# A Hyena block's transform step by half-height fp32 products from a turned x1

## The chip, the cores and the metric

The kernel runs on one core of a Trainium2 chip. The metric is the device time of one execution in microseconds (us). The engines are TensorE (PE), VectorE (DVE), ScalarE (ACT), GpSimd (POOL) and SyncE (SP, which issues DMAs here).

## The reference

One encoder layer on x of 2048 tokens by 1024 channels, all in float32. After an RMSNorm one projection gives 7168 columns, which feed two branches of 1024 channels:

```
a = c_val * sigmoid(c_gate);  a = depthwise conv of 31 taps over tokens
a = silu(layernorm per 128 channels(a)) * silu(c_z)
x0, x1, v = three depthwise convs of 3 taps
y = long_conv(v * x1) + skip;  y = rmsnorm per 128 channels(y * x0) * silu(hy_z)
out = rmsnorm(x + [a, y] @ w_out)
```

The long convolution is done by a transform of length 4096 in two steps. Its first step, the subject here, turns 2048 tokens, read as 64 rows n1 by 32 columns n2, into 32 vectors of 128 (64 real, 64 imaginary parts): for each n2, a product of a 64-row matrix of cosines and sines with the 64 tokens of that n2.

## The kernel before

A float32 product is written as three products of a faster format, fp32r: both operands are split into a high and a low part, and high by high, high by low and low by high are summed in PSUM (`chunk`, lines 235 to 237). 24 such products make one 128 by 512 output tile, here called a chunk, and four chunks (`inproj`) make one block of 128 projection columns for all tokens.

After the norm and the filters, phase A (about 400 to 1500 us) goes through eight groups of 128 channels. In turn i of its loop: `conf_glu(i)` projects value and gate (8 chunks) and writes the product into the buffer `apad`; `conf_taps(i)` runs the 31-tap convolution on DVE as 30 instructions of 128x2048 (line 541), given out a few at a time by `some(n)`; `conf_norm` centres the group before by products with `ctr` (lines 562 and 563, high and low part, which wait for ACT's L556 and DVE's L557) and gathers variances by four products on 32 columns of the array each (`vp`, line 569); `hyena(i - 1)` projects x1 and v, runs their short convolutions (`short_conv`: one ACT instruction L619, two DVE ones L621 and L622 per 512 tokens) and multiplies them (L640). Their sum `s` is a 128x2048 tile with tokens in order.

Then `stage1(i - 1)` does the transform's first step. It is a generator: `chunk` asks it for a step at two places of every chunk, while x0 and then the next gate are projected. A step takes the 64 tokens of a column n2 with a stride of 32, transposes them on PE (L662, four columns per PSUM bank), makes a high part by an ACT copy (L664) into partitions 0 to 63 and a low part by a DVE subtraction (L665) into partitions 64 to 127, and multiplies the stack by the 128-row matrix `st1`, in high and low part (L678, L679). ACT evicts the result (L681) and SP stores it to `AU` (L682).

The PSUM tiles `aux` (transposes, step results, centring) share three buffers, `mm` (chunks) has four; `apad` and `ppad` have one each. Each engine works through its own queue in order; a scheduler of the framework sets that order when the kernel is built, so it doesn't follow from the code alone. The view `turned` (tokens laid out column n2 by column) exists already for x0 and for the gate `hz`.

Of the kernel before, what the change touches and what calls it, by code (L numbers as in the profile page):

```python
# [11 lines left out]
F32 = mybir.dt.float32  # L12
F32R = mybir.dt.float32r
AF = mybir.ActivationFunctionType
# [4 lines left out]
P = 128  # L19
# [4 lines left out]
TC = 512  # L24
NT = L // TC
# [6 lines left out]
N1, N2 = 128, 32  # L32
# [27 lines left out]
def _split(m):  # L60

    m = np.asarray(m, np.float32)
    b = m.view(np.uint32)
    hi = ((b + np.uint32(0x7FF) + ((b >> np.uint32(12)) & np.uint32(1))) & np.uint32(0xFFFFF000)).view(np.float32)
    return hi, m - hi


def _constants():

    f32 = np.float32  # L70
    t = np.linspace(0.0, 1.0, L).astype(f32)
    bands = (EMB - 1) // 2
    w = f32(2.0 * math.pi / L) * np.arange(L, dtype=f32)
    f = np.linspace(1e-4, bands - 1, bands).astype(f32)
    fw = (f[None, :] * w[:, None]).astype(f32).astype(np.float64)
    z = np.concatenate([t[:, None], np.cos(fw).astype(f32), (-np.sin(fw)).astype(f32)], axis=1)

    fwd = np.empty((N2, 64), np.int64)
    bwd = np.empty((N2, 64), np.int64)
    for n2 in range(N2):  # L80
        fwd[n2] = 32 * np.arange(64) + n2
        bwd[n2] = 32 * (np.arange(64) + 1) - n2
    bwd[0, 63] = 0
    zf = np.concatenate([z[fwd.ravel()].T, z[bwd.ravel()].T], axis=0)
    tn = np.concatenate([-t[fwd].T, -t[bwd].T], axis=0)

    n1 = np.arange(N1)[:, None]
    k1 = np.arange(64)[None, :]
    ang = np.pi * (2 * k1 + 1) * n1 / 128.0
    e1 = np.concatenate([np.cos(ang), -np.sin(ang)], axis=1)  # L90
    s1u = np.concatenate([e1[:64], e1[:64]], axis=0)
    s1k = np.concatenate([e1[:64], -e1[128 - np.arange(1, 65)]], axis=0)
    s1k0 = s1k.copy()
    s1k0[127] = e1[0]
    st1 = np.stack([x for m in (s1u, s1k, s1k0) for x in _split(m.astype(f32))], axis=1)

    st2 = np.zeros((NPAIR, P, 8, P), f32)
    n2 = np.arange(N2)[:, None]
    k2 = np.arange(N2)[None, :]
    for p in range(NPAIR):  # L100
        m = np.zeros((2, 2, N2, 2, 2, N2))
        for l in range(2):
            kk = l * 32 + p
            g = np.exp(-1j * np.pi * ((2 * kk + 1) * n2 / 4096.0 + k2 * n2 / 16.0))
            m[0, l, :, 0, l, :] = g.real
            m[1, l, :, 0, l, :] = -g.imag
            m[0, l, :, 1, l, :] = g.imag
            m[1, l, :, 1, l, :] = g.real
        m = m.transpose(2, 0, 1, 3, 4, 5).reshape(P, P)
        re, im = m[:, :64], m[:, 64:]  # L110
        for j, x in enumerate((m, m.T, np.concatenate([re, re], axis=1), np.concatenate([-im, im], axis=1))):
            st2[p, :, 2 * j], st2[p, :, 2 * j + 1] = _split(np.ascontiguousarray(x).astype(f32))

    a = np.pi * (2 * np.arange(64)[:, None] + 1) * np.arange(64)[None, :] / 128.0
    inv = np.concatenate([np.cos(a), -np.sin(a)], axis=0) * (2.0 / 4096.0)
    sel = np.zeros((P, NT, P))
    for j in range(NT):
        sel[32 * j, j] = 1.0
        sel[32 * j + 16, j] = 1.0
    part = np.arange(P) % 32 >= 16  # L120
    ctr = np.eye(P) - np.full((P, P), 1.0 / P)
    return {
        "c_z": np.ascontiguousarray(zf),
        "c_t": np.ascontiguousarray(tn),
        "c_st1": np.ascontiguousarray(st1),
        "c_st2": st2,
        "c_inv": inv.astype(f32),
        "c_sel": sel.astype(f32),
        "c_part": np.stack([np.where(part, -1.0, 1.0), np.where(part, 1.0, 0.0)], axis=1).astype(f32),
        "c_ctr": ctr.astype(f32),  # L130
    }
# [39 lines left out]
def hybrid_kernel(ctx: ExitStack, tc: tile.TileContext, A, out):  # L171
    nc = tc.nc
    mm = nc.tensor.matmul
# [3 lines left out]
    AU = dram.tile([P, N2 + 1, D], F32, name="AU")  # L177
# [7 lines left out]
    cst = ctx.enter_context(tc.tile_pool(name="cst", bufs=1, reuse_waits="tile"))  # L185
# [6 lines left out]
    ident = cst.tile([P, P], F32, name="ident")  # L192
# [5 lines left out]
    nc.vector.memset(ones_g, 1.0 / P)  # L198
    ctr = cst.tile([P, P], F32R, name="ctr")
    sel = cst.tile([P, NT, P], F32R, name="sel")  # L200
    st1 = cst.tile([P, 2, P], F32R, name="st1")

# [37 lines left out]
    with ExitStack() as c0:  # L242
        hzp = c0.enter_context(tc.tile_pool(name="hzp", bufs=2, reuse_waits="tile"))
        ps = c0.enter_context(tc.tile_pool(name="ps0", bufs=1, space=PSUM, reuse_waits="tile"))
# [77 lines left out]
        for i, k in ((1, EMB), (2, FO), (3, FO)):  # L322
            w = kp.tile([2 * k, P], F32, name=f"fw{i}")
# [8 lines left out]
        for c in range(2):  # L332
# [2 lines left out]
            nc.sync.dma_start(wo_raw, A["filt_wo"][:, cs])  # L335
            nc.vector.tensor_copy(woh[:, cs], wo_raw)
            nc.vector.tensor_sub(wol[:, cs], wo_raw, woh[:, cs].bitcast(F32))
        for to, name, w in ((ctr, "c_ctr", P), (sel.rearrange("p a b -> p (a b)"), "c_sel", NT * P),
                            (st1.rearrange("p a b -> p (a b)"), "c_st1", 2 * P)):
            raw = kp.tile([P, TC], F32, name="dec", bufs=2)[:, :w]  # L340
            src = A[name] if name == "c_ctr" else A[name].rearrange("p a b -> p (a b)")[:, :w]
            nc.sync.dma_start(raw, src)
            nc.vector.tensor_copy(to, raw)
        stk = kp.tile([P, 4, P], F32R, name="stk")
        sk_raw = kp.tile([P, 4, P], F32, name="dec", bufs=2)
        nc.sync.dma_start(sk_raw, A["c_st1"][:, 2:6])
        nc.vector.tensor_copy(stk, sk_raw)

        def mlp(t):
# [107 lines left out]
    def tmp(dt=F32, shape=(P, TC)):  # L457
        return wk.tile(list(shape), dt, name="t", bufs=NTMP)
# [39 lines left out]
    with ExitStack() as c0:  # L498
        ps = c0.enter_context(tc.tile_pool(name="psA", bufs=1, space=PSUM, reuse_waits="tile"))
# [92 lines left out]
        def turned(x):  # L592

            return x.rearrange("p (n2 n1) -> p n1 n2", n2=N2)
# [18 lines left out]
        def short_conv(co, a, j, turn=False):  # L613
            n = TC

            def v(x):
                return x.rearrange("p (a b) -> p a b", b=N2) if turn else x

            nc.scalar.activation(co, v(ppad[:, a + 1:a + 1 + n]), AF.Identity, bias=sm("sh_b", j),  # L619
                                 scale=sm("sh_w", 3 * j + 1))  # L620
            nc.vector.scalar_tensor_tensor(co, v(ppad[:, a:a + n]), sm("sh_w", 3 * j), co, op0=OP.mult, op1=OP.add)  # L621
            nc.vector.scalar_tensor_tensor(co, v(ppad[:, a + 2:a + 2 + n]), sm("sh_w", 3 * j + 2), co,  # L622
                                           op0=OP.mult, op1=OP.add)

        def x1_out(i, some):
            s = long()

            def conv(t):
                short_conv(s[:, t * TC:(t + 1) * TC], t * TC, 8 + i)
                some(1)  # L630

            short_in(32 + i, after=conv)
            return s

        def gated(s, i, some):
            def conv(t):
                ts = slice(t * TC, (t + 1) * TC)
                c = tmp()
                short_conv(c, t * TC, 16 + i)
                nc.vector.tensor_mul(s[:, ts], s[:, ts], c)  # L640

            short_in(40 + i, after=conv)

# [10 lines left out]
            return c  # L654

        def stage1(i, s, some):
            sv = s.rearrange("p (n1 n2) -> p n2 n1", n2=N2)

            def turn(q):
                tp = ps.tile([64, 4, P], F32, name="aux", bufs=3)  # L660
                for r in range(4):
                    nc.tensor.transpose(tp[:, r], sv[:, 4 * q + r], ident)  # L662
                S = tmp(F32R, (P, 4, P))
                nc.scalar.activation(S[:64], tp, AF.Copy)  # L664
                nc.vector.tensor_sub(S[64:], tp, S[:64].bitcast(F32))  # L665
                return S

            for _ in range(STAGE1_WAIT):
                yield
            S = [turn(0)]  # L670
            yield
            S.append(turn(1))
            yield
            for q in range(8):
                if q < 6:
                    S.append(turn(q + 2))
                so = ps.tile([P, 4, P], F32, name="aux", bufs=3)
                mm(so, st1[:, 0], S[q], start=True, stop=False)  # L678
                mm(so, st1[:, 1], S[q], start=False, stop=True)  # L679
                sb = tmp(F32, (P, 4, P))  # L680
                nc.scalar.activation(sb, so, AF.Copy)  # L681
                nc.sync.dma_start(AU[:, 4 * q:4 * q + 4, i * P:(i + 1) * P], sb)  # L682
                if q % 2:
                    some(1)
                yield

        def hyena(i, some):
# [6 lines left out]
        for i in range(NG):  # L694
# [4 lines left out]
            def some(n):  # L699
                for _ in range(n):  # L700
                    next(taps, None)
# [124 lines left out]
    with ExitStack() as c0:  # L826
        f1 = c0.enter_context(tc.tile_pool(name="f1", bufs=1, reuse_waits="tile"))
        fp = c0.enter_context(tc.tile_pool(name="fp", bufs=1, reuse_waits="tile"))
        ps = c0.enter_context(tc.tile_pool(name="psB", bufs=1, space=PSUM, reuse_waits="tile"))
# [230 lines left out]
```

## Time and profile before

| | |
|---|---|
| median of three runs | 2160.95 us (2158.88 to 2162.77) |
| profiled execution | 2159.41 us, of which the span is 2157.7 us |
| PE busy | 2076.8 us, 96% of the span |
| DVE busy | 1581.6 us, 73% |
| ACT busy | 1127.2 us, 52% |
| granted clock of PE, mean | 0.99 |

In the rows below, a duration of a PE instruction holds the depth of its pipeline, so the price of one in a stream is the distance between two starts. "x4" at the end of a row means four instructions in a run. In square brackets stands how long the engine had been idle before, and what ended that.

### The profile page before, as it was taken

To read this page: it belongs to the slowest core of one execution; us is meant where nothing else is said; L and a number is where in the kernel's file an instruction comes from. 1 tells how busy PE (TensorE), PEld (TensorE's weight loads), DVE (VectorE), ACT (ScalarE), POOL (GpSimd) and SP (SyncE) were. 2 spreads that over 40 slices of the span, in tenths; PEclk is the share of its full clock that TensorE was granted. 3 is DMA by queue.
4 is the path that set the end of the run, shared out by engine and by line. 5 is a ranking of instruction groups with operands and counts; after the bars stand their busy time and mean duration, and the time that the engine had idled before them with its cause. 6 is when DMAs were issued, how large, how long until landed. Compare 5 with 4: busy or idle time off the path is not lost. (4 is left out here: it accounts for less than half of the span.)

```text
span 2157.7 us, 23506 instructions
## 1 busy us (share of the span) xinstructions
PE 2076.8 (96%) x9076; PEld 1617.5 (75%) x9076; DVE 1581.6 (73%) x1519; ACT 1127.2 (52%) x1663; POOL 25.3 (1%) x52
## 2 busy tenths in 40 slices
PE   6999999999999999999999999999999999999998
PEld 5677788887887887877878878777777776666666
DVE  5687639498597695994994976986787886375664
ACT  6488712333434433433344344447898997365662
POOL 0000000000000000000000000001000000000000
PEclk9999999999999999999999999999999999999999
DMA  8433311112112202212121121127877786776652
GB/s 311 157 116 147 140 37 52 67 59 74 45 69 78 78 25 74 78 35 92 60 67 51 65 77 54 59 79 251 298 267 259 262 277 229 254 205 185 186 159 66
DMA packets 157104, 277.34 MB, mean 129 GB/s; under 512 B 11062, under 2 KB 93366, under 8 KB 151872
## 3 DMA queue, kind: packets, MB, share of 16 engines
q1 hardware_dynamic: 151008, 253.82, 35.8%
q0 software_dynamic: 5984, 22.02, 3.3%
q8 instruction: 71, 1.16, 0.2%
q14 instruction: 41, 0.34, 0.0%
HBM read 175.14 MB, written 100.66 MB: 128 GB/s over the span
## 5 line engine op out<-in xcount | busy, mean ns | idle before, releaser
L235 PE MATMUL mm<-uh,wh 128*128 128x512 f32 x1792 | 709.8, 397 | 6.8 <-ACT wh L226 3.5
L236 PE MATMUL mm<-ul,wh 128*128 128x512 f32 x1792 | 705.4, 394 | 1.6 <-DVE ul L296 1.6
L237 PE MATMUL mm<-uh,wl 128*128 128x512 f32 x1792 | 705.4, 394 | 0.3 <-DVE wl L228 0.3
L541 DVE SCALAR_TENSOR_TENSOR long<-apad,small,long 128x2048 f32<-128x2048 f32 x240 | 562.7, 2344 | 9.2 <-ACT long L538 6.7
L235 PEld LDWEIGHTS mm<-uh,wh 128*128 128x128 f32 x1792 | 340.3, 190 | 88.9 <-DVE apad L533 5.9
L236 PEld LDWEIGHTS mm<-ul,wh 128*128 128x128 f32 x1792 | 340.2, 190 | 77.7 <-DVE ul L296 3.6
L237 PEld LDWEIGHTS mm<-uh,wl 128*128 128x128 f32 x1792 | 339.8, 190 | 74.8 <-issue 1.6
L608 ACT ACTIVATE ppad<-mm 128x512 f32<-128x512 f32 x96 | 57.3, 597 | 224.6 <-PE mm L237 203.0
L783 PE MATMUL o<-wo,ml 128*128 128x512 f32 x384 | 152.2, 396 | 0.0
L781 PE MATMUL o<-wo,mh 128*128 128x512 f32 x384 | 152.0, 396 | 0.0
L782 PE MATMUL o<-wo,mh 128*128 128x512 f32 x384 | 151.9, 396 | 0.0
L226 ACT ACTIVATE wh<-wr 128x1024 fp32r<-128x1024 f32 x56 | 59.3, 1060 | 154.7 <-PE mm L236 147.4
L533 DVE TENSOR_TENSOR apad<-mm,apad 128x512 f32<-128x512 f32 x32 | 22.1, 692 | 154.7 <-PE mm L237 154.7
L228 DVE TENSOR_TENSOR wl<-wr,wh 128x1024 fp32r<-128x1024 f32 x56 | 68.3, 1220 | 53.7 <-ACT wh L226 52.7
L664 ACT ACTIVATE t<-aux 64x512 fp32r<-64x512 f32 x64 | 37.8, 594 | 103.5 <-PE aux L662 103.5
L782 PEld LDWEIGHTS o<-wo,mh 128*128 128x128 f32 x384 | 72.2, 188 | 18.9 <-issue 3.3
L783 PEld LDWEIGHTS o<-wo,ml 128*128 128x128 f32 x384 | 72.2, 188 | 18.1 <-issue 2.9
L781 PEld LDWEIGHTS o<-wo,mh 128*128 128x128 f32 x384 | 72.2, 188 | 17.0 <-issue 1.2
L564 ACT ACTIVATE long<-aux 128x512 f32<-128x512 f32 x32 | 19.0, 594 | 101.3 <-PE aux L563 101.3
L619 ACT ACTIVATE long<-ppad,small 128x512 f32<-128x512 f32 x64 | 68.8, 1076 | 1.9
L621 DVE SCALAR_TENSOR_TENSOR long<-ppad,small,long 128x512 f32<-128x512 f32 x64 | 66.8, 1046 | 0.7 <-ACT long L619 0.5
L681 ACT ACTIVATE t<-aux 128x512 f32<-128x512 f32 x64 | 37.7, 590 | 55.6 <-PE aux L679 55.4
(217 smaller groups left out, 3116.8 us busy)
## 6 DMA issues: line engine op xcount, KB each, us to landing
wr<-in_w_in_dram SPq DMA_DIRECT2D x56, 512.0 KB, 3.6
AK<-ak SPq DMA_DIRECT2D x64, 256.0 KB, 2.0
AU<-t SPq DMA_DIRECT2D x64, 256.0 KB, 2.3
au<-AU SPq DMA_DIRECT2D x32, 512.0 KB, 4.6
g<-in_c_st_dram POOLq DMA_DIRECT2D x32, 512.0 KB, 5.9
ak<-AK SPq DMA_DIRECT2D x32, 512.0 KB, 5.3
VD<-vs SPq DMA_DIRECT2D x32, 512.0 KB, 5.3
long<-VD SPq DMA_DIRECT2D x16, 1024.0 KB, 5.3
```

What stands on the lines that cost most here:

```text
L226: nc.scalar.activation(wh, wr, AF.Copy)
L228: nc.vector.tensor_sub(wl, wr, wh.bitcast(F32))
L235: mm(pt, wh[:, k], uh[t][:, k], start=(k == 0), stop=False)
L236: mm(pt, wh[:, k], ul[t][:, k], start=False, stop=False)
L237: mm(pt, wl[:, k], uh[t][:, k], start=False, stop=(k == KT - 1))
L541: nc.vector.scalar_tensor_tensor(acc, apad[:, j:j + L], sm("dw_w", i * CK + j), acc, op0=OP.mult, op1=OP.add)
L608: nc.scalar.activation(ppad[:, 1 + t * TC:1 + (t + 1) * TC], pt, AF.Copy)
L619: nc.scalar.activation(co, v(ppad[:, a + 1:a + 1 + n]), AF.Identity, bias=sm("sh_b", j), scale=sm("sh_w", 3 * j + 1))
L621: nc.vector.scalar_tensor_tensor(co, v(ppad[:, a:a + n]), sm("sh_w", 3 * j), co, op0=OP.mult, op1=OP.add)
L781: mm(o, mh[:, k], wh[:, cs], start=(k == 0), stop=False)
L782: mm(o, mh[:, k], wl[:, cs], start=False, stop=False)
L783: mm(o, ml[:, k], wh[:, cs], start=False, stop=(k == KT - 1))
```

## The change

The step is done on all 128 partitions. x1's convolution writes `s` in the turned layout, and the gate multiply reads and writes it so (both by strided accesses of 16 by 32); v's convolution stays plain. A transpose now takes 128 neighbouring entries of `s`, which are the 64 tokens of two columns n2, so 16 transposes of 128 entries stand where 32 of 64 stood. ACT copies a bank of four once, as float32, all 128 partitions; there is no split and no DVE subtraction. The product with the matrix is a plain float32 one of 64 rows: the upper half of the partitions gives one set of columns n2, the lower half the other, each into a PSUM bank of its own. The matrix `st1` is loaded as it is, in one more small DMA at the start. All line numbers behind the change are one higher.

```diff
-    st1 = cst.tile([P, 2, P], F32R, name="st1")
+    st1 = cst.tile([P, P], F32, name="st1")
...
+        nc.sync.dma_start(st1, A["c_s1u"])
...
             def conv(t):
-                short_conv(s[:, t * TC:(t + 1) * TC], t * TC, 8 + i)
+                short_conv(turned(s)[:, 16 * t:16 * (t + 1)], t * TC, 8 + i, turn=True)
                 some(1)
...
                 c = tmp()
                 short_conv(c, t * TC, 16 + i)
-                nc.vector.tensor_mul(s[:, ts], s[:, ts], c)
+                to = turned(s)[:, 16 * t:16 * (t + 1)]
+                nc.vector.tensor_mul(to, to, c.rearrange("p (a b) -> p a b", b=N2))
...
             def turn(q):
-                tp = ps.tile([64, 4, P], F32, name="aux", bufs=3)
-                for r in range(4):
-                    nc.tensor.transpose(tp[:, r], sv[:, 4 * q + r], ident)
-                S = tmp(F32R, (P, 4, P))
-                nc.scalar.activation(S[:64], tp, AF.Copy)
-                nc.vector.tensor_sub(S[64:], tp, S[:64].bitcast(F32))
+
+                tp = ps.tile([P, 4, P], F32, name="aux", bufs=3)
+                for j in range(4):
+                    at = (8 * q + 2 * j) * 64
+                    nc.tensor.transpose(tp[:, j], s[:, at:at + P], ident)
+                S = tmp(F32, (P, 4, P))
+                nc.scalar.activation(S, tp, AF.Copy)
                 return S
...
-            for q in range(8):
-                if q < 6:
-                    S.append(turn(q + 2))
-                so = ps.tile([P, 4, P], F32, name="aux", bufs=3)
-                mm(so, st1[:, 0], S[q], start=True, stop=False)
-                mm(so, st1[:, 1], S[q], start=False, stop=True)
-                sb = tmp(F32, (P, 4, P))
-                nc.scalar.activation(sb, so, AF.Copy)
-                nc.sync.dma_start(AU[:, 4 * q:4 * q + 4, i * P:(i + 1) * P], sb)
-                if q % 2:
-                    some(1)
+            for q in range(4):
+                now = S
+                if q < 3:
+                    S = turn(q + 1)
+                    yield
+                so = [ps.tile([P, 4, P], F32, name="aux", bufs=3) for r in range(2)]
+                for r in range(2):
+                    rs = slice(64 * r, 64 * (r + 1))
+                    mm(so[r], st1[rs], now[rs], start=True, stop=True)
+                for r in range(2):
+                    sb = tmp(F32, (P, 4, P))
+                    nc.scalar.activation(sb, so[r], AF.Copy)
+                    nc.sync.dma_start(AU[:, bass.ds(8 * q + r, 4, step=2), i * P:(i + 1) * P], sb)
+                some(1)
                 yield
```

The order of the instructions follows. On PE, in the first turn that has a step, the kernel before reads (t is the split stack, aux a PSUM bank, 12 products of a chunk stand at each "...")

```order
L662 MATMUL aux_3811<-ident_76,long_3432 64x128 x4
L678 MATMUL aux_3819<-t_3770,st1_88 128x512
L679 MATMUL aux_3819<-t_3770,st1_88 128x512
...
L662 MATMUL aux_3837<-ident_76,long_3432 64x128 x4
L678 MATMUL aux_3845<-t_3790,st1_88 128x512
L679 MATMUL aux_3845<-t_3790,st1_88 128x512
```

and the changed one

```order
L680 MATMUL aux_3807<-t_3768,st1_88 128x512
L680 MATMUL aux_3808<-t_3768,st1_88 128x512
...
L663 MATMUL aux_3830<-ident_76,long_3430 128x128 x4
...
L680 MATMUL aux_3866<-t_3787,st1_88 128x512
L680 MATMUL aux_3867<-t_3787,st1_88 128x512
```

A transposition and a product no longer stand together, and there are half as many transposes; each L680 is one float32 product.

On DVE, at the end of the same turn's taps, the kernel before has subtractions between the last taps (long with apad) and behind the weight split L228, ahead of the centring's split L557

```order
L541 SCALAR_TENSOR_TENSOR long_3273<-apad_2398,small_75,long_3273 128x2048
L665 TENSOR_TENSOR t_3886<-aux_3881,t_3886 64x512
L541 SCALAR_TENSOR_TENSOR long_3273<-apad_2398,small_75,long_3273 128x2048
L665 TENSOR_TENSOR t_3912<-aux_3907,t_3912 64x512
L541 SCALAR_TENSOR_TENSOR long_3273<-apad_2398,small_75,long_3273 128x2048
L228 TENSOR_TENSOR wl_3928<-wr_3924,wh_3926 128x1024
L665 TENSOR_TENSOR t_3946<-aux_3941,t_3946 64x512
L665 TENSOR_TENSOR t_3972<-aux_3967,t_3972 64x512
L557 TENSOR_TENSOR t_4024<-long_3273,t_4023 128x512
```

and the changed one

```order
L542 SCALAR_TENSOR_TENSOR long_3271<-apad_2396,small_75,long_3271 128x2048 x2
L229 TENSOR_TENSOR wl_3902<-wr_3898,wh_3900 128x1024
L623 SCALAR_TENSOR_TENSOR long_3690<-ppad_2399,small_75,long_3690 128x16x32
L622 SCALAR_TENSOR_TENSOR long_3690<-ppad_2399,small_75,long_3690 128x16x32
L542 SCALAR_TENSOR_TENSOR long_3271<-apad_2396,small_75,long_3271 128x2048
L623 SCALAR_TENSOR_TENSOR long_3690<-ppad_2399,small_75,long_3690 128x16x32
L542 SCALAR_TENSOR_TENSOR long_3271<-apad_2396,small_75,long_3271 128x2048 x2
L558 TENSOR_TENSOR t_3978<-long_3271,t_3977 128x512
```

The weight split has moved ahead of the last three taps, and the centring's split follows the last tap directly.

On ACT, the sigmoid of the next gate (L527, which writes `apad` and so must follow the last tap) stands, before, so to the step's evictions L681 and the centring's copy L556:

```order
L681 ACTIVATE t_3978<-aux_3975 128x512
L527 ACT_TABLE_LOAD
L527 ACTIVATE apad_2398<-mm_3871 128x512
L527 ACTIVATE apad_2398<-mm_3931 128x512
L681 ACTIVATE t_3998<-aux_3995 128x512
L681 ACTIVATE t_4016<-aux_4013 128x512
L556 ACTIVATE t_4023<-long_3273 128x512
```

and now

```order
L683 ACTIVATE t_3919<-aux_3915 128x512
L528 ACT_TABLE_LOAD
L528 ACTIVATE apad_2396<-mm_3856 128x512
L683 ACTIVATE t_3922<-aux_3916 128x512
L683 ACTIVATE t_3941<-aux_3937 128x512
L683 ACTIVATE t_3944<-aux_3938 128x512
L557 ACTIVATE t_3977<-long_3271 128x512
```

Three evictions of the step stand between the first sigmoid and the centring's copy, where two sigmoids and two evictions stood.

## Rows read from the trace of the kernel before

**Rows 1.** Windows from stall to stall, five groups: length, busy time and (count) by engine
```profile
sum 744.90, PE 723.81 PEld 591.04 DVE 591.24 ACT 297.30 POOL 0.00; mean PE 144.76 PEld 118.21 DVE 118.25 ACT 59.46 POOL 0.00
```

**Rows 2.** Waits of PE, 200 to 1500 us: total us, times, longest us
```profile
PE aux L678 <- DVE t L665: 28.9, 9, 4.2
```

**Rows 3.** Timeline of PE at the fifth stall: start us, us, engine, line, [idle before]
```profile
1122.81 0.80 PE L678 MATMUL aux<-t,st 128*128 128x512 f32 x1 [4.21 <-DVE t L665]
```

**Rows 4.** Timeline of DVE at the same place
```profile
1119.68 2.36 DVE L541 SCALAR_TENSOR_TENSOR long<-apad,small,long 128x2048 f32<-128x2048 f32 x1
1122.07 0.69 DVE L665 TENSOR_TENSOR t<-aux,t 64x512 fp32r<-64x512 f32 x1
```

**Rows 5.** Windows of 10 us behind two stalls; PEclk is the third number from the end
```profile
526.10:536.10 10.00, 9.91 (x33) 7.87 (x34) 7.93 (x7) 3.74 (x6) 0.00 (x0) 0.69 0.36 100
...
1122.80:1132.80 10.00, 9.99 (x39) 8.18 (x40) 7.79 (x6) 4.64 (x7) 0.00 (x0) 0.83 0.46 139
```

**Rows 6.** Timeline of PE at the first transposes of group 5
```profile
1096.71 0.39 PE L237 MATMUL mm<-uh,wl 128*128 128x512 f32 x1
1096.94 0.60 PE L662 MATMUL aux<-ident,long 128*64 128x128 f32 x4
...
1097.61 0.39 PE L236 MATMUL mm<-ul,wh 128*128 128x512 f32 x1
```

**Rows 7.** Timeline of PE at full-row fp32 products and at the four column-tiled ones
```profile
82.86 1.88 PE L355 MATMUL st<-ht,fw 66*128 66x512 f32 x4
...
84.80 0.39 PE L236 MATMUL mm<-ul,wh 128*128 128x512 f32 x1
...
1016.28 0.39 PE L237 MATMUL mm<-uh,wl 128*128 128x512 f32 x1
1016.59 1.06 PE L569 MATMUL vp<-long,ones_g 128*32 128x512 f32 x8
...
1017.93 0.39 PE L236 MATMUL mm<-ul,wh 128*128 128x512 f32 x1
```

**Rows 8.** Timeline of DVE: plain forms, then the subtraction and two turned forms
```profile
1075.88 0.74 DVE L621 SCALAR_TENSOR_TENSOR t<-ppad,small,t 128x512 f32<-128x512 f32 x1
1076.54 0.68 DVE L640 TENSOR_TENSOR long<-long,t 128x512 f32<-128x512 f32 x1
1077.14 2.34 DVE L541 SCALAR_TENSOR_TENSOR long<-apad,small,long 128x2048 f32<-128x2048 f32 x1
...
1090.51 2.34 DVE L541 SCALAR_TENSOR_TENSOR long<-apad,small,long 128x2048 f32<-128x2048 f32 x1
...
1104.21 0.68 DVE L665 TENSOR_TENSOR t<-aux,t 64x512 fp32r<-64x512 f32 x1
1104.93 1.34 DVE L622 SCALAR_TENSOR_TENSOR long<-ppad,small,long 128x512 f32<-128x512 f32 x1
1106.18 1.37 DVE L621 SCALAR_TENSOR_TENSOR long<-ppad,small,long 128x512 f32<-128x512 f32 x1
```

**Rows 9.** Timelines of DVE, ACT and PE from the last taps to the variance
```profile
1128.16 1.22 DVE L228 TENSOR_TENSOR wl<-wr,wh 128x1024 fp32r<-128x1024 f32 x1
...
1135.22 0.60 ACT L681 ACTIVATE t<-aux 128x512 f32<-128x512 f32 x1 [2.65 <-PE aux L679]
1135.72 0.62 ACT L556 ACTIVATE t<-long 128x512 fp32r<-128x512 f32 x1
...
1141.35 0.39 PE L563 MATMUL aux<-t,ctr 128*128 128x512 f32 x1
...
1164.88 1.07 PE L569 MATMUL vp<-long,ones_g 128*32 128x512 f32 x8
```

**Rows 10.** Timelines of DVE and PE at the end of the last period
```profile
1439.61 1.23 DVE L228 TENSOR_TENSOR wl<-wr,wh 128x1024 fp32r<-128x1024 f32 x1 [2.30 <-ACT wh L226]
...
1443.35 0.68 DVE L557 TENSOR_TENSOR t<-long,t 128x512 fp32r<-128x512 f32 x1
...
1444.09 0.49 PE L563 MATMUL aux<-t,ctr 128*128 128x512 f32 x1
```

More of the change, by code (lines that the diff above doesn't have):

```diff
@@ L94, in _constants @@
     s1k0[127] = e1[0]
-    st1 = np.stack([x for m in (s1u, s1k, s1k0) for x in _split(m.astype(f32))], axis=1)
+    st1 = np.stack([x for m in (s1k, s1k0) for x in _split(m.astype(f32))], axis=1)
     st2 = np.zeros((NPAIR, P, 8, P), f32)
@@ L124, in _constants @@
         "c_t": np.ascontiguousarray(tn),
+        "c_s1u": s1u.astype(f32),
         "c_st1": np.ascontiguousarray(st1),
@@ L337, in hybrid_kernel @@
             nc.vector.tensor_sub(wol[:, cs], wo_raw, woh[:, cs].bitcast(F32))
-        for to, name, w in ((ctr, "c_ctr", P), (sel.rearrange("p a b -> p (a b)"), "c_sel", NT * P),
-                            (st1.rearrange("p a b -> p (a b)"), "c_st1", 2 * P)):
+        for to, name, w in ((ctr, "c_ctr", P), (sel.rearrange("p a b -> p (a b)"), "c_sel", NT * P)):
             raw = kp.tile([P, TC], F32, name="dec", bufs=2)[:, :w]
@@ L345, in hybrid_kernel @@
         sk_raw = kp.tile([P, 4, P], F32, name="dec", bufs=2)
-        nc.sync.dma_start(sk_raw, A["c_st1"][:, 2:6])
+        nc.sync.dma_start(sk_raw, A["c_st1"])
+        nc.sync.dma_start(st1, A["c_s1u"])
         nc.vector.tensor_copy(stk, sk_raw)
@@ L636, in conv @@
             def conv(t):
-                ts = slice(t * TC, (t + 1) * TC)
                 c = tmp()
                 short_conv(c, t * TC, 16 + i)
-                nc.vector.tensor_mul(s[:, ts], s[:, ts], c)
+                to = turned(s)[:, 16 * t:16 * (t + 1)]
+                nc.vector.tensor_mul(to, to, c.rearrange("p (a b) -> p a b", b=N2))
             short_in(40 + i, after=conv)
@@ L656, in stage1 @@
         def stage1(i, s, some):
-            sv = s.rearrange("p (n1 n2) -> p n2 n1", n2=N2)
             def turn(q):
-                tp = ps.tile([64, 4, P], F32, name="aux", bufs=3)
-                for r in range(4):
-                    nc.tensor.transpose(tp[:, r], sv[:, 4 * q + r], ident)
-                S = tmp(F32R, (P, 4, P))
-                nc.scalar.activation(S[:64], tp, AF.Copy)
-                nc.vector.tensor_sub(S[64:], tp, S[:64].bitcast(F32))
+                tp = ps.tile([P, 4, P], F32, name="aux", bufs=3)
[4 more added lines that the diff above has]
+                nc.scalar.activation(S, tp, AF.Copy)
                 return S
@@ L669, in stage1 @@
                 yield
-            S = [turn(0)]
+            S = turn(0)
             yield
-            S.append(turn(1))
-            yield
-            for q in range(8):
-                if q < 6:
-                    S.append(turn(q + 2))
-                so = ps.tile([P, 4, P], F32, name="aux", bufs=3)
-                mm(so, st1[:, 0], S[q], start=True, stop=False)
-                mm(so, st1[:, 1], S[q], start=False, stop=True)
-                sb = tmp(F32, (P, 4, P))
-                nc.scalar.activation(sb, so, AF.Copy)
-                nc.sync.dma_start(AU[:, 4 * q:4 * q + 4, i * P:(i + 1) * P], sb)
-                if q % 2:
-                    some(1)
+            for q in range(4):
[12 more added lines that the diff above has]
+                some(1)
                 yield
```

## The prediction

> **What bounds the kernel now.** I read the page first: PE is busy 96% of the span, so time can only go where PE idles, runs slowly or does needless work. The windows from one turn of phase A to the next then show what a turn is made of: 744.9 us over five turns, 149.0 each, with PE busy 144.8 and DVE 118.3 [rows 1]. The waits of PE name one place: L678 waits nine times, 28.9 us, for the subtraction L665 on DVE, 4.2 us at most [rows 2]. The timeline of PE at the fifth of these gives 4.21 us at once, at the fifth of the step's eight products [rows 3]; five other turns show the same, so three short waits in the last turn share 28.9 - 6 x 4.2 = 3.7 us. The timeline of DVE there says why: the subtraction, 0.7 us long, stood behind a tap of 2.3 us and what was before it [rows 4]. DVE is full up to its last tap and idles afterwards, so it is late in one half of a turn and early in the other. What the stall costs beyond itself stands in the clock: in the 10 us behind it the granted clock averages 0.69 to 0.83 (these are the lowest and the highest of six; part of the time PE is at 1.2 GHz instead of 2.4) [rows 5]. That is 1.7 to 3.1 us of work lost each time, 2.4 over the six.
>
> **PE's part of a turn.** Between 1096.71 and 1097.61 PE starts a chunk product, four transposes and one more product; less two products at 0.23 that is 0.44 for four transposes [rows 6]. 16 fewer save 1.8 us (I charge 128 columns like 64, since the price is the row streaming through). The 16 fp32r products of the old step go, at 0.23: 3.7 us. The stall goes, 4.2, and its clock, 2.4.
>
> Added are four pairs of fp32 products of 64 rows, which this trace doesn't have. Bounds: four instructions of full-height fp32, two products, take 84.80 - 82.86 - 0.23 = 1.71 us, so one product is two passes of 0.43 [rows 7]. Four fp32 products on 32 columns each, eight instructions, take 1017.93 - 1016.28 - 0.46 = 1.19 us [rows 7]: they run side by side in the time of one (0.86), plus 0.33 for changing the array's division and back. A pair thus costs 0.86 at least, 1.71 + 0.33 = 2.04 at most. I take 1.19, the row of a divided array, 4.8 us a turn. The sum for PE is -4.2 - 2.4 - 1.8 - 3.7 + 4.8 = -7.3, a turn of 141.7 us if PE had nothing to wait for.
>
> A rule speaks against this. The Trainium skill, "TensorE: Matmul & The Clock Gate", "What overlaps and what doesn't", has products start and end strictly in program order. By it the second half's first pass would come behind the first half's second, three passes instead of two, and the four column products of the rows would need five. The trace disagrees for column halves; no run so far shows row halves. What this would make of the time is among the rivals, from the passes of the rows.
>
> **DVE's and ACT's part.** x1's eight convolution instructions become turned ones: plain 1076.54 - 1075.88 = 0.66, turned 1106.18 - 1104.93 = 1.25 [rows 8], so 8 x 0.59 = 4.7 us. The multiply is 0.60 plain (1077.14 - 1076.54) [rows 8]. A turned multiply isn't in the trace: at least 0.60, and no row caps it. It too reads and writes one strided operand, so I take the turned row's doubling: 1.2, 4 x 0.6 = 2.4 us. Together DVE comes 7.1 us later to the end of the multiplies. Before, it was done at 1090.5 and PE wanted its first transposes at 1096.94, 6.4 us later [rows 6, 8]; the cover is gone and PE waits 0.7 us there.
>
> Six of the eight subtractions stood ahead of the last tap, 6 x 0.72 = 4.3 us gone (1104.93 - 1104.21) [rows 8]. The weight split, 1.2 us, moves ahead of it. The last tap, which ended at 1128.16 when that split began [rows 9], now ends at 1128.2 + 7.1 - 4.3 + 1.2 = 1132.2. Behind it ACT's queue has the first sigmoid, three evictions and only then the centring's copy: four times 0.5 (1135.72 - 1135.22) [rows 9], 0.6 for the copy, 0.7 for DVE's split [rows 9, 10]: 3.3 us. The centring's low product can go at 1135.5, against 1141.35 before; PE would be there at 1141.35 - 7.3 + 0.7 = 1134.7. It waits 0.8 us, and from there to the variance are 1164.88 - 1141.35 = 23.5 us of products that the change doesn't touch [rows 9]. From the variance at 1016.59 [rows 7] to the next at 1159.0 it is 142.4 us, by DVE, and 142.4 by PE with its wait. So a turn shrinks by 6.6 us, six turns by 39.6, and DVE's queue has become as tight as PE.
>
> ACT saves four copies a turn and pays the turned form in x1; it stands at 297.3 / 5 = 59 of 149 us [rows 1] and hides both. The stores to AU are as many as before, equally large and later waited for only by phase B. The one new DMA lies in SP's queue at the start, beside the norm.
>
> **The end of phase A.** In the last turn DVE works for two groups before the centring: +7.1 and -5.8 (eight subtractions) for the one, +4.7 and +1.8 (three multiplies) for the other. 2.3 us of that fill a wait of DVE for the weight copy [rows 10], so its first split moves from 1443.35 by +5.5, and with it the centring's low product at 1444.09 [rows 10]. PE, relieved of 3.7 us of waits, arrives some 5 us earlier than before and waits about 10 us; the half clock behind such a wait I charge with 1.7, the least that a stall cost. That is +7.2. The last group's step has no taps beside it: PE saves 0.7 and its pairs, now back to back, wait for ACT's evictions about as much. In all 2159.4 - 39.6 + 7.2 = 2127 us, against the profiled execution's own time; it lies 1.5 below the median of the three runs, inside their spread.
>
> **Rivals.**
> *The halves don't overlap.* One behind the other, a pair costs 2.04, 3.4 us more a turn: PE's turn is 145.1 + 0.7, six gain 19, the end loses 8: 2148. In strict order with three passes, 1.28 + 0.33 = 1.61, it is 144.1, six gain 29, the end loses 7.5: 2137. For it: no row has row halves. Against: the column products overlap fully. 0.12 and 0.10.
> *DVE keeps up.* If the turned multiply costs no more than a plain one, DVE comes only 4.7 us later, the cover of 6.4 holds, and PE alone sets 141.7: six gain 43.8, the end loses 2: 2117. Against: the turned convolution did double. 0.12.
> *The turned multiply is far dearer: slower.* Each 1 us beyond 1.2 adds 4 us to six turns and about 7 to the last, where two groups' multiplies stand ahead of the centring: 31 us. The gain of 32 is gone at 2.25 us an instruction; at 2.6 the time is 2170. For it: two operands and the result of a two-tensor operation with strides, a form without a row. Against: the convolution's instruction is one too, and costs 1.25. 0.05.
> *The wait stays, in another dress:* the unsplit copy stands in ACT's queue behind evictions into `ppad` that wait for DVE, so the product still waits 4.2 us and pays the clock. Then -7.3 becomes -0.7 a turn and the end's loss stays: about 2162. Against: ahead of the copies ACT's queue has only evictions whose buffers DVE has long left. 0.04.
>
> **How the numbers follow.** 0.57 for the forecast, whose own range is 2120 to 2135 by the price of the pair and of the multiply. The rivals on the fast side reach from 2117 to 2148; with the lower bound of a pair (0.86) and DVE out of the way the time would be some 2 to 4 us below 2117. So 2113 to 2148 leaves the last two rivals out, and a little beyond. A change of under 0.2%, 4 us, could not be told from none. Faster 0.91; the case of the staying wait lies about half within 4 us, so 0.02 for the same; slower 0.07.
>
> **What would show it.** Right: no wait of 4 us for DVE at the products of the step; a clock near full behind them; the pair in about 1.2 us from chunk product to chunk product, its four instructions in two passes; the turned multiply 1.2 us apart from what follows; variances 142 to 143 us apart; PE waiting under 1 us at the centring in six turns and about 10 in the last. Wrong: pairs of 1.6 or 2.0 us, a multiply over 2 us, a wait of PE at the first transposes of several us, or a centring that waits long enough to lose the clock again in every turn.

## The result

The changed kernel takes 2133.44 us (median of four runs, 2130.54 to 2133.78) against 2160.86 of the kernel before (four runs, the three known before and one more): 0.987 of it, 95% interval 0.9853 to 0.9887. The forecast was 2127, its own range 2120 to 2135. Its profiled execution took 2133.78 us, with a span of 2132.0.

The windows from the first variance product of one turn (`vp`, L570) to that of the next give the seven turns that follow. A row has start and end, length, the busy times in the order of [rows 1], and, third from the end, PE's granted clock:

```profile
421.17:563.95 142.78, 141.97 (x629) 112.83 (x628) 119.28 (x82) 59.16 (x78) 0.00 (x0) 1.00 0.21 67
...
1135.12:1277.88 142.76, 141.97 (x630) 112.83 (x629) 119.28 (x82) 59.19 (x78) 0.00 (x0) 1.00 0.20 67
1277.88:1415.42 137.54, 129.86 (x556) 101.44 (x555) 135.66 (x98) 60.70 (x77) 1.75 (x3) 0.98 0.19 62
```

Six turns are 142.8 us long where 149.0 stood, PE is busy 142.0 of it, and the granted clock is 1.00 throughout. DVE is about as busy as before, 119.3 where 118.3 stood: what the subtraction gave, the turned forms took. The last turn has grown. PE's waits in phase A, to be set beside [rows 2]:

```profile
PE aux L663 <- DVE long L641: 4.8, 6, 0.8
PE mm L238 <- DVE wl L229: 3.8, 1, 3.8
PE aux L563 <- ACT t L557: 2.7, 1, 2.7
PE aux L680 <- ACT t L683: 1.9, 3, 1.3
PE aux L564 <- DVE t L558: 0.8, 2, 0.5
```

The 28.9 us for L665 are gone. What came is the small wait for the gate product at the first transposes, once in each of six turns, and, in the last turn and behind it, the four rows below that one. In the turn from 992.33 the timeline of PE has the first transposes with their wait, and then the first pair of half products between two chunk products, with no wait:

```profile
1073.63 0.66 PE L663 MATMUL aux<-ident,long 128*128 128x128 f32 x4 [0.79 <-DVE long L641]
...
1079.85 0.39 PE L238 MATMUL mm<-uh,wl 128*128 128x512 f32 x1
1080.16 1.13 PE L680 MATMUL aux<-t,st 64*128 64x512 f32 x4
...
1081.56 0.39 PE L237 MATMUL mm<-ul,wh 128*128 128x512 f32 x1
```

The pair costs 1081.56 - 1079.85 - 2 x 0.23 = 1.25 us, near the 1.19 of the column-tiled products in [rows 7]. At the end of the taps, where [rows 9] stood, DVE and PE read:

```profile
1102.81 4.75 DVE L542 SCALAR_TENSOR_TENSOR long<-apad,small,long 128x2048 f32<-128x2048 f32 x2
1110.19 0.69 DVE L558 TENSOR_TENSOR t<-long,t 128x512 fp32r<-128x512 f32 x1 [2.64 <-ACT t L557]
...
1111.35 0.40 PE L563 MATMUL aux<-t,ctr 128*128 128x512 f32 x1
1111.59 0.39 PE L564 MATMUL aux<-t,ctr 128*128 128x512 f32 x1
```

DVE's split is done at 1110.9, PE comes for the low product (L564) at 1111.6 and doesn't wait.

### The profile page after: what moved, and what is told of

Its sections match the earlier page's. It is cut to its first block, busy times and chain, and to the rows that moved or that the text cites. A ratio compares the mean times of both kernels' runs of the same rounds, so it can differ in the third digit from the quotient of the medians.

```text
span 2132.0 us, 23126 instructions
## 1 busy us (share of the span) xinstructions
PE 2067.2 (97%) x8948; PEld 1586.1 (74%) x8948; DVE 1589.5 (75%) x1454; ACT 1123.4 (53%) x1631; POOL 25.3 (1%) x52
## 5 line engine op out<-in xcount | busy, mean ns | idle before, releaser
L229 DVE TENSOR_TENSOR wl<-wr,wh 128x1024 fp32r<-128x1024 f32 x56 | 68.6, 1225 | 39.1 <-ACT wh L227 38.2
L622 DVE SCALAR_TENSOR_TENSOR long<-ppad,small,long 128x512 f32<-128x512 f32 x64 | 85.4, 1336 | 5.1 <-ACT long L620 5.0
L623 DVE SCALAR_TENSOR_TENSOR long<-ppad,small,long 128x512 f32<-128x512 f32 x64 | 86.0, 1343 | 0.1
L620 ACT ACTIVATE long<-ppad,small 128x512 f32<-128x512 f32 x64 | 84.7, 1324 | 2.0
L528 ACT ACTIVATE apad<-mm 128x512 f32<-128x512 f32 x32 | 19.6, 617 | 83.6 <-DVE long L542 70.3
```

What stands on the lines that cost most here:

```text
L229: nc.vector.tensor_sub(wl, wr, wh.bitcast(F32))
```

## The experiments

All eight kernels in one table. Behind the median, each column is from one profile: the mean distance of first variance products over six turns ("a turn"), the last such distance, from there to the first output product ("then"), and from the first to the last output product ("rest", code that no kernel here touches).

| kernel | median us | a turn | last turn | then | rest |
|---|---|---|---|---|---|
| before | 2160.86 | 149.0 | 131.7 | 54.9 | 648.4 |
| changed | 2133.44 | 142.8 | 137.5 | 56.5 | 651.4 |
| turned_alone | 2211.76 | 155.8 | 143.1 | 54.9 | 649.6 |
| no_subtraction | 2119.38 | 142.3 | 127.4 | 54.6 | 652.0 |
| halves_apart | 2162.15 | 148.0 | 138.0 | 56.9 | 646.6 |
| x1_plain | 2113.82 | 141.75 | 127.0 | 54.9 | 647.6 |
| last_group_plain | 2127.57 | 142.8 | 132.7 | 56.5 | 649.4 |
| x1_plain_swapped | 2115.86 | 141.75 | 127.9 | 54.9 | 649.2 |

The question was where the gain comes from. Theory: from DVE's queue, by the stall and its clock, with PE's own saving near nothing and the turned forms a loss. Rival: from fewer transposes and products on PE, with the turned forms hidden.

**turned_alone**, the dear half of the change put into the kernel before:

```diff
-                short_conv(s[:, t * TC:(t + 1) * TC], t * TC, 8 + i)
+                short_conv(turned(s)[:, 16 * t:16 * (t + 1)], t * TC, 8 + i, turn=True)
...
-                nc.vector.tensor_mul(s[:, ts], s[:, ts], c)
+                to = turned(s)[:, 16 * t:16 * (t + 1)]
+                nc.vector.tensor_mul(to, to, c.rearrange("p (a b) -> p a b", b=N2))
...
-                    nc.tensor.transpose(tp[:, r], sv[:, 4 * q + r], ident)
+                    nc.tensor.transpose(tp[:, r], s[:, (4 * q + r) * 64:(4 * q + r + 1) * 64], ident)
```

> The kernel before with one part of the change: x1 and the gate product in the turned layout, the 64-column transposes reading it without a stride; split, subtraction and fp32r products stay. Theory (DVE's queue decides): 7.1 us more of DVE work ahead of the step's subtractions in every turn, so the wait of 4.2 us grows to about 11, spread over several products, and the clock falls more often; a turn of 149 becomes 156 to 158 us, the whole about 2205 to 2220. Rival (the turned forms lie beside PE and cost nothing): 2160.

2211.76 us, 1.0238 of before (1.0221 to 1.0255). Its waits of PE in phase A:

```profile
PE aux L679 <- DVE t L666: 54.9, 15, 4.6
PE aux L663 <- DVE long L641: 5.0, 6, 0.9
PE mm L237 <- DVE wl L228: 3.8, 1, 3.8
```

L666 is the subtraction and L679 the product behind it: 54.9 us in fifteen waits where 28.9 in nine stood. A turn is 155.8 us where 156 to 158 were expected, 6.8 longer than before: the 7.1 us of DVE work appear almost whole. The turned layout alone is a loss of 51 us.

**no_subtraction**, the cheap half alone (the low part of the split is left out):

```diff
-                nc.vector.tensor_sub(S[64:], tp, S[:64].bitcast(F32))
+                nc.scalar.activation(S[64:], tp, AF.Copy)
```

> The kernel before with one part of the change: DVE's subtraction is gone, a second ACT copy of the transposed bank stands for the low part (so the low part is left out of the computation). PE's transposes and products stay. Theory (the gain is the stall on DVE with its clock): a turn falls from 149.0 to about 142.4 us, the last turn loses its 3.7 us of waits, the whole is 2112 to 2120, faster than the changed kernel. Rival (the gain came from fewer transposes and products on PE): 2145 or more.

2119.38 us, 0.9813 (0.9798 to 0.9827). With all the old transposes and fp32r products in place, a turn falls by 6.7 us to 142.3. That is the 4.2 of the stall, and the 2.5 by which PE's busy time fell, from 144.8 [rows 1] to 142.3 with the same products at a clock of 1.00; PE is busy without a gap:

```profile
991.30:1133.60 142.30, 142.30 (x649) 116.56 (x648) 112.55 (x82) 64.31 (x90) 0.00 (x0) 1.00 0.20 67
```

So the rival falls: the step's work on PE didn't have to change for the gain.

**halves_apart**, the pair's overlap taken away:

```diff
                 for r in range(2):
+                    if r:
+                        yield
                     rs = slice(64 * r, 64 * (r + 1))
                     mm(so[r], st1[rs], now[rs], start=True, stop=True)
```

> The changed kernel with the two half products of a pair put apart by one step of the generator, twelve chunk products between them. Theory (halves run side by side, a pair takes 1.26 us from chunk product to chunk product): a lone half costs nearly what a pair costs, 4 x 1.2 = 4.8 us more a turn, 147 us, the whole about 2160. Rival (the halves run one behind the other, the change-over is small): about 2134 to 2140.

2162.15 us (ten runs, 1.0011 of before, 1.0002 to 1.002). The timeline of PE at a lone half:

```profile
1101.86 0.39 PE L238 MATMUL mm<-uh,wl 128*128 128x512 f32 x1
1102.17 1.12 PE L682 MATMUL aux<-t,st 64*128 64x512 f32 x2
...
1103.56 0.39 PE L237 MATMUL mm<-ul,wh 128*128 128x512 f32 x1
```

1103.56 - 1101.86 - 0.46 = 1.24 us for one half, 1.25 for two: the halves run fully side by side, and without that the change would have gained nothing. By strict program order, as the prediction took it from the Trainium skill, "TensorE: Matmul & The Clock Gate", "What overlaps and what doesn't", a pair would have been one pass of 0.43 dearer than a lone half; here it isn't. The same figures refute the rival with a pair of 1.61.

**x1_plain**, the changed kernel without most of the turned work:

```diff
-            s = long()
+            s = []
...
-                short_conv(turned(s)[:, 16 * t:16 * (t + 1)], t * TC, 8 + i, turn=True)
+                s.append(tmp())
+                short_conv(s[t], t * TC, 8 + i)
...
-        def gated(s, i, some):
+        def gated(x1, i, some):
+            s = long()
...
-                nc.vector.tensor_mul(to, to, c.rearrange("p (a b) -> p a b", b=N2))
+                nc.vector.tensor_mul(to, x1[t].rearrange("p (a b) -> p a b", b=N2),
+                                     c.rearrange("p (a b) -> p a b", b=N2))
...
```

> The changed kernel with x1's convolution plain again, into four small tiles; the gate product reads both operands plain and writes the turned layout. Theory: 4.7 us less on DVE ahead of the step, so the wait of 0.8 us at the first transposes goes and a turn is PE's 142.0; the last turn, where DVE carries two groups, gains some 5 to 8; the whole 2120 to 2126. If the product is dear because of its strided write alone it stays at 1.2 us; if because of its strided read, it falls to 0.6. Rival (DVE is not what the turn or the end waits for): 2133.

2113.82 us, 0.9787 (0.9772 to 0.9801): faster than both kernels, by 47 and 20 us, and faster than the 2120 to 2126 expected. The six turns gave 6.2 us back and not 4.8, the last one 10.5 and not 5 to 8; 1.6 more lie behind it, in the clock (at the end of this text), and a net 1.6 in code that the edit doesn't touch. A turn is 141.75 us, and PE is busy all of it:

```profile
990.30:1132.05 141.75, 141.75 (x633) 112.89 (x632) 113.74 (x82) 57.30 (x78) 0.00 (x0) 1.00 0.20 67
1273.80:1400.80 127.00, 126.47 (x556) 99.60 (x555) 124.36 (x97) 56.46 (x77) 1.12 (x2) 1.00 0.20 67
```

Against no_subtraction's 142.3 that is 0.55 us: what the step's new products and fewer transposes save on PE. So the change's 6.2 us a turn are 6.7 for the stall and its clock and 0.55 for PE's work, less 1.0 (142.78 - 141.75) for the wait that the turned forms cause. The gate product, with plain reads and a strided write, is neither 0.6 nor 1.2 but between, 1051.13 - 1050.22 = 0.91 us:

```profile
1050.22 1.09 DVE L644 TENSOR_TENSOR long<-t 128x512 f32<-128x512 f32 x1
1051.13 2.33 DVE L542 SCALAR_TENSOR_TENSOR long<-apad,small,long 128x2048 f32<-128x2048 f32 x1
```

**last_group_plain**, x1_plain's edit under `if i == NG - 1` alone, to split the last turn's 10.5 us.

> The changed kernel with x1's convolution plain for the last of the eight groups alone (four small tiles, product as in x1_plain); the other seven stay turned. Theory (in the last turn DVE carries two groups' dearer work before the centring, and the end waits for that sum): the six turns stay at 142.8 us; in the last, 8 x 0.59 for the convolution and 3 x 0.27 for the products are gone, so of the 10.5 us that x1_plain gained there 5.5 come back and the rest, from the seventh group's turned work, stays; the whole about 2126 to 2128. Rival (the last group's own work is the whole of it): 2121 to 2123.

2127.57 us, 0.985 (0.9836 to 0.9865); the last turn 132.7, so 4.8 of the 10.5 us belong to the last group and the rest to the group before it. PE's waits there show what remains:

```profile
PE aux L671 <- DVE long L648: 5.0, 6, 0.9
PE mm L238 <- DVE wl L229: 3.8, 1, 3.8
PE aux L688 <- ACT t L691: 1.9, 3, 1.3
```

The waits at the centring are gone, the 3.8 us for the weights' low part (L229) stay. They go with the seventh group's turned convolution, whose eight DVE instructions stand ahead of L229: that split starts 48.8 us behind the turn's first variance here and in the changed kernel, 44.1 before and in x1_plain, where the row is missing. The difference is the 8 x 0.59 of those instructions. In the changed kernel:

```profile
1326.66 1.23 DVE L229 TENSOR_TENSOR wl<-wr,wh 128x1024 fp32r<-128x1024 f32 x1
```

**x1_plain_swapped**, x1_plain with the product's loops exchanged:

```diff
-                to = turned(s)[:, 16 * t:16 * (t + 1)]
-                nc.vector.tensor_mul(to, x1[t].rearrange("p (a b) -> p a b", b=N2),
-                                     c.rearrange("p (a b) -> p a b", b=N2))
+                to = s.rearrange("p (n2 n1) -> p n2 n1", n2=N2)[:, :, 16 * t:16 * (t + 1)]
+                nc.vector.tensor_mul(to, x1[t].rearrange("p (a b) -> p b a", b=N2),
+                                     c.rearrange("p (a b) -> p b a", b=N2))
```

> x1_plain with the gate product's two loops exchanged: the write then goes in runs of 16 neighbours, both reads have a stride of 32 elements. In x1_plain, whose write alone is strided, the product took 0.92 us from start to start, in the changed kernel with a strided read more 1.17, in the kernel before 0.60. Theory (each strided operand adds about 0.3 us, whichever it is): about 1.2 us. Rival (writes in runs are free and the two reads share one price): 0.9. Either way PE sets the turn in x1_plain, DVE has room, and the time stays within 0.2% of x1_plain's, about 2114.

2115.86 us, 0.9799 (0.9783 to 0.9816), not told apart from x1_plain; its last turn, though, is 0.9 us longer, and PE waits 1.1 us for DVE's split at the centring there, so in that turn DVE has no room left. Two strided reads and a write in runs of 16 cost 1050.81 - 1049.69 = 1.12 us, about what the theory said:

```profile
1049.69 1.22 DVE L644 TENSOR_TENSOR long<-t 128x512 f32<-128x512 f32 x1
1050.81 2.36 DVE L542 SCALAR_TENSOR_TENSOR long<-apad,small,long 128x2048 f32<-128x2048 f32 x1
```

## Why the prediction was right, and where it missed

From 2157.7 to 2132.0 the span fell by 25.7 us; 32.4 were forecast. By parts of the trace:

| part | forecast | measured |
|---|---|---|
| up to the first variance | 0 | +1.2 |
| six turns | -39.6 | -37.4 |
| last turn and what follows, to the first output product | +7.2 | +5.9 + 1.7 |
| rest | 0 | +3.0 |

*The stall and its clock* were sized right: 4.2 + 2.4 forecast, 6.7 measured alone by no_subtraction (the six clocks behind the stalls, 0.69 to 0.83, give 2.5 and not 2.4).

*PE's own work* was right in kind. It was to save 1.8 + 3.7 - 4.8 = 0.7 us a turn; no_subtraction and x1_plain differ by 0.55. The term that was sized too low is the pair, 1.25 for 1.19, 0.24 us a turn; the other two came out 0.1 better together. Four transposes of 128 columns cost 0.44 us in x1_plain (1071.29 - 1070.39 - 0.46), as four of 64 did. "PE alone" was forecast as 141.7 and is 141.75 in x1_plain.

*The turned layout.* Eight convolution instructions at +0.59 and the product at 1.2 held: in the changed kernel a product takes 1062.25 to 1063.42, 1.17 us.

```profile
1062.25 1.28 DVE L641 TENSOR_TENSOR long<-long,t 128x512 f32<-128x512 f32 x1
1063.42 4.74 DVE L542 SCALAR_TENSOR_TENSOR long<-apad,small,long 128x2048 f32<-128x2048 f32 x2
```

The wait at the first transposes, 0.7 forecast, is 0.8. But it costs more than its length: with it a turn is 142.78 us, without it, in x1_plain, 141.75. These 1.03 for 0.7, with 0.05 from PE's work, are the 0.4 by which a turn is longer than forecast.

*The tie of DVE and PE* is the step that failed. I had the centring wait 0.8 us for DVE in each turn. The last tap ends 1107.5 - 992.33 = 115.2 us behind the turn's first variance, forecast 1132.2 - 1016.6 = 115.6, so DVE came a little earlier, PE a little later, and nothing waits. The turn is PE's work and the wait at the transposes, not DVE's queue at the centring: 142.8 for 142.4. A slip in the sum made the wait: the turn that it was worked from is 1164.88 - 1016.59 = 148.3 us long [rows 7, 9], not the mean's 149.0, and its stall cost 1.7 us of clock (0.83 in [rows 5]), not 2.4. With its own 1.7, PE would have been forecast at 1135.4 beside DVE's 1135.5.

*The last turn.* DVE's first split of the centring was to come 5.5 us later; it moved from 1443.35 - 1314.05 = 129.3 us behind the turn's first variance (the first row below, and [rows 10]) to 1412.47 - 1277.88 = 134.6 (the second row), by 5.3:

```profile
1314.05 1.06 PE L569 MATMUL vp<-long,ones_g 128*32 128x512 f32 x8
...
1412.47 0.69 DVE L558 TENSOR_TENSOR t<-long,t 128x512 fp32r<-128x512 f32 x1
```

But PE's wait isn't one of ten us at the centring. The first 3.8 us of it stand early in the turn, at a chunk product that needs L229, which I hadn't looked for, and the rest in three parts:

```profile
1327.94 0.80 PE L238 MATMUL mm<-uh,wl 128*128 128x512 f32 x1 [3.79 <-DVE wl L229]
...
1408.60 0.51 PE L563 MATMUL aux<-t,ctr 128*128 128x512 f32 x1 [2.75 <-ACT t L557]
...
1413.22 0.49 PE L564 MATMUL aux<-t,ctr 128*128 128x512 f32 x1 [0.48 <-DVE t L558]
...
1414.99 0.49 PE L564 MATMUL aux<-t,ctr 128*128 128x512 f32 x1 [0.35 <-DVE t L558]
```

DVE's queue sets this turn: it is busy for 135.7 of the 137.5 us. So the early wait costs nothing of its own here, since without it PE would have come to the centring sooner and waited there. last_group_plain, where DVE is in time for the centring, pays for it: 3.8 us, and 1.7 in the 10 us behind it at a clock of 0.83, of the 5.7 us by which its last turn is longer than x1_plain's.

*What follows the last turn* was to be even and lost 1.7 us, by the clock behind the last pair's wait for ACT (below). The forecast's +7.2 held 1.7 for the clock behind the centring's wait; the last turn itself grew by 5.9, only 0.6 more than DVE's split moved. That 7.6 came out beside 7.2 is luck.

*Outside phase A* 4.2 of the 6.7 missing us lie in code that the change doesn't touch, but for one small DMA. Over the eight profiles the first variance lies between 419.6 and 423.3 us and the rest takes 646.6 to 652.0, with no order by kernel, so I take these for the scatter between runs, which one profile of each kernel can't prove. Most of it is PE at work for longer and not more waiting: from the first to the last output product it is busy 630.9 us against 628.7 before, up to the first variance 399.7 against 398.3, with as many products (2716 and 2717, 1696 and 1696). Whether the DMA for `st1` has a share in the first 1.2 us stays open: the five kernels with it have 421.2 to 423.3, the three without 419.6 to 422.1.

The rivals: halves one behind the other, in full or by one pass, and the staying wait are refuted by the pair's 1.25 us with halves_apart, and by the waits. A far dearer product didn't come. "DVE keeps up" is the state that x1_plain brings about, with 2114 where 2117 stood.

## What to carry to other kernels

When an engine stalls on one late instruction in another's queue, price the change by that queue: here moving the subtraction away gave 6.7 us a turn, the rebuilt product half a microsecond. Ask of every helper edit what it adds to the queue that was late: the new layout gave 20 of a possible 47 us back (some 17 of them in the seven turns), and only its write was needed. And look at the turn that differs from the others, the last one, by itself, with every instruction behind the dearer ones, weight preparation too.

## What the runs showed of the hardware

A 128x512 product of two float32 tensors on DVE takes 0.60 us from start to start with all operands plain [rows 8], 0.91 with a strided write (x1_plain), 1.17 with one strided read and a strided write (the changed kernel; a step of 64 elements in these two), and 1.12 with two strided reads (a step of 32) and a write in runs of 16 (x1_plain_swapped). No row shows how the last splits between its reads and its write.

Two 64-row float32 products on the halves of the array take 1.25 us between fp32r products (the changed kernel), and one takes 1.24 (halves_apart).

The clock doesn't follow from the length of a wait alone. Behind the same wait of 1.3 us for ACT at the last pair the granted clock was 0.83 over ten us in the changed kernel

```profile
1445.40:1455.40 10.00, 8.70 (x25) 5.58 (x26) 3.46 (x4) 3.98 (x8) 3.81 (x8) 0.83 1.05 347
```

and full in x1_plain, whose PE ran the same instructions ahead of it:

```profile
1430.80:1440.80 10.00, 8.70 (x33) 5.75 (x34) 3.40 (x4) 5.13 (x10) 3.83 (x8) 1.00 1.05 352
```

That is 0.17 x 10 = 1.7 us, the step from 54.9 to 56.5 in the table. last_group_plain (0.83 over the ten us) and x1_plain_swapped (1.00) have the same wait and differ in the same way. An earlier fall isn't what tells them apart: last_group_plain, like x1_plain, had a clock of 1.00 over the 30 us ahead. What decides it these runs don't show.
